# A mixer layer on one core: buffers of four head merges laid elsewhere, and the attention gates kept in halves

## The chip, the cores and the metric

The kernel runs on one core of one Trainium2 chip. The time is what the device needs for one execution, in microseconds (us). The kernel before was timed in three runs: 884.32, 889.29 and 890.98 us, median 889.29. A further run was executed with the hardware profiler on; all rows of the profile come from that one execution.

## The reference, cut to what matters

One layer mixes 1024 latent tokens (width 1024, a grid of 16 rows and 64 columns) with the help of 256 context tokens. It is computed in float32.

```python
h = rmsnorm(x, g_pre) * (1 + scale) + shift          # scale, shift, gate from c (and c_ctx for the context)
na_q, na_k, na_v, na_z, g_qkv, g_z, g_b, g_a = split(h @ w_in)
o_na = neighborhood_attention(na_q, na_k, na_v, ctx_k, ctx_v, rpb)      # 8 heads of 64
q, k, v = l2norm/silu(short_conv(g_qkv)); q, k = axial_rope(q), axial_rope(k)
beta, g = sigmoid(g_b), -exp(A_log) * softplus(g_a + dt_bias)
# gated delta rule, 4 heads of 128, both directions; per chunk of tokens:
a = tril(kb @ k.T * decay, -1);  t_inv = inv(I + a)
u = t_inv @ (v * beta);  w = t_inv @ (kb * exp(gc))
o_g = scan over chunks (state, u, w, q, k), forward + backward
y = concat([o_na * silu(na_z), rmsnorm(o_g) * silu(g_z)]) @ w_out
out = x + gate * rmsnorm(y, g_post)
```

## The kernel before, in words

Every large product is made as three float32r products of high and low parts, so that TensorE works most of the time. The kernel has four stages.

1. **Input and projections** (`phase0`, `phase2`). The modulated input lies transposed in SBUF. Projections of the delta branch go through a short convolution (`conv`, L857, tiles `xp`, `acc`), then to token tiles (`qk_tok`, `qk_back`); `delta_front` (L1004) makes per head the matrices `pm` and `qe` and writes them to DRAM. All these tiles lie in the pool `cv`. A unit triangular 128x128 matrix per head, direction and chunk has to be inverted: `delta_front` copies its four 32x32 diagonal blocks to `ab_dram`, and `inv_blocks` (L1058) inverts them on VectorE (DVE) in 31 steps of two instructions (L1070, L1073). The 320 blocks are handled in three groups (g = 0, 1, 2). Groups 0 and 1 are done within stage 1, group 2 in the next stage; its results go to DRAM as `yd2`, and head 3 alone needs them.

2. **The merges** (`phase_a2`, L1432). While the last projections of the attention (pairs 2 and 3: `pq`, `pk`, `pz`) still run on TensorE (PE), `inv_merge` (L1081) puts the inverted blocks of each of the four heads h together to 128x128 inverses. Its steps are l (load `pmf` from `pm_dram`, and `vl` from `yd`), t (three transposes on DVE: `vx` L1106, `vd` L1107, `ld` L1108, copies into `tm` on ScalarE), z (products `tz`, L1120), u (products `tu`, L1139, whose negatives DVE puts into `tm` and `xo`, L1144), w (products `tz2`, L1153) and e (products `tu2`, results by L1163 and L1164 into `tm`, then two DMAs to `tm_dram`, L1166). The list `MERGES` (L138) gives the order of the steps over the heads. `tm` for direction 0 alternates between `tms[0]` and `tms[1]`; direction 1 has `tms[2]` for all heads, so a head's first write into it waits until the DMA of the head before has read it. `phase_a2` also loads the first attention pair (`na_load`, L562: `kk`, `qh`, `ql`, `gt`, `vv` and the mask `mk`).

3. **Attention and scan** (`phase_b`, L1484). The attention runs in four pairs of heads p = 0 to 3, each in two halves of the queries, rt = 0 and 1, and each half in four column tiles ct. `na_scores`, `na_turn` and `na_values` make the scores, their transposes and the products with the values, which add up in the PSUM tile `po` (one buffer). After the fourth column tile `values` (L620) multiplies the gate tile `zs` by `po` (L627), and `end` (L636) multiplies it by the transposed reciprocal sums, the PSUM tile `prt` (L640, L642), which takes the one buffer of `po` in turn. The result goes to `m_dram` (L646); that of pair 3 stays in SBUF and is split into high and low parts by `split_m` (L708). `zs` is a tile of 1024 queries with one buffer, so pair p + 1 can load it only when both halves of pair p have been written out. Between the attention steps the delta scan (`delta_step`) is called, head by head; `delta_end` (L1293) of a head writes its gated output `zg` to `m_dram` (L1319).

4. **Output projection** (`phase4`): products `py` (L1361 to L1363) over the eight parts k of the mixed width in the order `W_ORDER`, and `out_tile`. Part k = 3 is the result of pair 3.

Engines take their instructions in the order in which the program has them. That order is made by a scheduler of the tile framework, which puts the instructions of each engine in an order by its own estimate of the times; `self.pe` and `self.order` pin some of it. All DMAs above are issued by SyncE (SP), one after the other: a DMA whose buffer isn't free holds all that stand behind it. Pools lie at fixed places in SBUF. The pool `pf` (pair 0 and 2, and borrowed by the merges) and the pool `a2` of the merges (the argument `g3` of `inv_merge`) lie where `cv` was: `a2` takes the addresses where the convolutions' tiles `xp`, `acc` and the token tiles were, the middle and upper parts of `pf` those where the last head's `em`, `pm` and `qe` tiles of `delta_front` were.

## Time and profile before

| | |
|---|---|
| three runs, median | 889.29 us (884.32 to 890.98) |
| the profiled execution | 885.84 us, its span 884.1 us, so 1.7 us outside the span |
| PE busy, share of the span | 829.0 us, 94% |
| DVE, ACT (ScalarE), POOL (GpSimd) | 57%, 47%, 40% |
| granted TensorE clock, mean | 0.968 |
| DMA | 159.65 MB, 181 GB/s on average |

How it is read. PE is busy for 94% of the span, so what a change can give back is for the most part the remaining 55 us in which PE waits, and the time in which PE runs at a lower granted clock. A row of a chain or of waits names what ended a wait; a row of the timeline has the start, the duration, the engine and line, the operation with its tiles, and, in brackets, the idle time before it with what ended it. `SPq` rows are DMAs being issued; the time in them is the issue, not the transfer.

### The profile page before, as it was taken

How to read it: one execution, taken by the hardware profiler on the slowest of the kernel's cores; microseconds unless marked ns; L12 is line 12 of the kernel's file. 1: busy time of each engine (PE TensorE's matmuls, PEld its weight loads, DVE VectorE, ACT ScalarE, POOL GpSimd, SP SyncE). 2: the span in 40 equal slices, each digit the busy share in tenths (PEclk: the TensorE clock that was granted, in tenths of full speed). 3: DMA queues.
4: the chain of work that ended last, by engine and by line, in shares of the span. 5: the costliest groups of instructions: out<-in, count | busy, mean ns of one | idle time of the engine just before them, and what ended most of it. 6: DMA issues, size and time to landing. Idle time of an engine off the chain costs nothing.

```text
span 884.1 us, 16449 instructions
## 1 busy us (share of the span) xinstructions
PE 829.0 (94%) x6082; PEld 701.9 (79%) x6082; DVE 507.9 (57%) x1050; ACT 417.9 (47%) x1086; POOL 357.3 (40%) x430
## 2 busy tenths in 40 slices
PE   5999999999999989898998998999889898989996
PEld 4678887888788768688886887898888787878885
DVE  3454465546626699869819944466466466663342
ACT  5353435744653643464315433666556566753110
POOL 1333231634463461426452103657547468624110
PEclk9999999999999999999998997899999999999999
DMA  9787442264464626543696499986919715123251
GB/s 332 263 274 271 131 132 86 84 214 151 117 204 156 182 85 198 172 121 82 232 244 218 159 265 340 359 190 244 269 56 297 209 60 204 49 108 131 76 194 65
DMA packets 85046, 159.65 MB, mean 181 GB/s; under 512 B 18261, under 2 KB 45222, under 8 KB 82790
## 3 DMA queue, kind: packets, MB, share of 16 engines
q1 hardware_dynamic: 77478, 144.94, 51.4%
q10 hardware_dynamic: 7488, 13.67, 4.8%
q8 instruction: 48, 0.79, 0.4%
q14 instruction: 32, 0.26, 0.1%
HBM read 109.51 MB, written 52.42 MB: 183 GB/s over the span
## 4 chain that ended last, share of the span: by engine, by line
PE 64%; DVE 16%; DMA 13%; issue 3%; ACT 2%; SPq 1%; POOL 0%; DVEq 0%; POOLq 0%; ACTq 0%
PE py L1361 3%; PE py L1362 3%; PE py L1363 3%; DVE tb L1070 3%; DVE vb L1073 2%; PE pa L1252 2%; PE pz L468 2%; PE pz L467 2%; PE pz L463 2%; DMA pm_dram<-pm 2%; PE pa L1263 2%; PE po L781 2%; PE sc L746 2%; DMA tm_dram<-tm 2%; PE po L776 2%
## 5 line engine op out<-in xcount | busy, mean ns | idle before, releaser
L751 ACT ACTIVATE pt<-pt,nm 128x544 f32<-128x544 f32 (+1 forms) x64 | 50.5, 790 | 47.6 <-DVE nm L750 47.3
L750 DVE CUSTOM_DVE_ANT_0 pt<-sc,gm 128x544 f32<-128x544 f32 (+1 forms) x64 | 49.3, 771 | 29.9 <-PE sc L746 25.0
L734 POOL TENSOR_TENSOR gm<-gt,mk 128x288 f32<-128x288 f32 (+1 forms) x48 | 46.5, 972 | 28.7 <-DVE nm L750 28.4
L1224 POOL TENSOR_SCALAR kd<-kt,kd 128x128 f32<-128x128 f32 x72 | 42.7, 605 | 20.6 <-PE pa L1263 19.5
L1012 ACT ACTIVATE em<-em,gc 128x128 f32<-128x128 f32 x80 | 25.5, 391 | 35.3 <-DMA em<-gc_dram 25.8
L467 PE MATMUL pz<-hl,wh_gz 128*128 128x512 f32 x96 | 38.6, 402 | 0.0
L1423 DVE TENSOR_TENSOR finv<-py,ggb 128x512 f32<-128x512 f32 x16 | 10.8, 688 | 47.9 <-ACT finv L1422 47.7
L463 PE MATMUL pz<-hh,wh_gz 128*128 128x512 f32 x96 | 38.3, 399 | 0.0
L468 PE MATMUL pz<-hh,wl_gz 128*128 128x512 f32 x96 | 38.3, 399 | 0.0
L476 PE MATMUL pv<-wh_nv,hh 128*128 128x264 f32 x128 | 35.3, 295 | 2.0 <-ACT hh L265 1.7
L1266 DVE SCALAR_TENSOR_TENSOR s<-s,egl,pa 128x128 f32<-128x128 f32 x64 | 19.7, 344 | 29.3 <-PE pa L1263 29.3
L477 PE MATMUL pv<-wh_nv,hl 128*128 128x264 f32 x128 | 36.5, 290 | 0.0
L1230 POOL TENSOR_SCALAR vb<-v,beta 128x128 f32<-128x128 f32 x40 | 24.2, 604 | 29.9 <-DVE y L1236 27.2
L1031 POOL TENSOR_SCALAR_AFFINE_SELECT qe<-qe 128x256 f32<-128x256 f32 x32 | 25.5, 799 | 25.0 <-DVE qe L1030 24.6
L478 PE MATMUL pv<-wl_nv,hh 128*128 128x264 f32 x128 | 35.4, 286 | 0.0
L879 DVE SCALAR_TENSOR_TENSOR acc_v<-xp_v,cols,acc_v 128x1282 f32<-128x1282 f32 x16 | 29.1, 1817 | 10.8 <-ACT acc_v L877 10.6
L1070 DVE TENSOR_TENSOR tb<-ab,vb 120x31 f32<-120x31 f32 (+15 forms) x62 | 30.2, 487 | 8.6 <-DMA ab<-ab_dram 7.0
L1422 ACT ACTIVATE finv<-py 128x512 f32<-128x512 f32 x16 | 9.5, 598 | 52.9 <-PE py L1363 34.8
L1129 POOL COPY tm<-ld 32x320 f32<-32x320 f32 x16 | 7.3, 454 | 64.1 <-DMA tm_dram<-tm 50.4
L1027 DVE SCALAR_TENSOR_TENSOR pm<-pk,beta,em 128x128 f32<-128x128 f32 x80 | 23.6, 342 | 15.2 <-PE pk L1020 11.0
L764 PE MATMUL tr<-c,pt 128*96 128x128 f32 (+1 forms) x192 | 31.8, 275 | 0.0
L1073 DVE TENSOR_TENSOR vb<-vb,tb 120x31 f32<-120x31 f32 (+15 forms) x62 | 30.1, 486 | 1.6
(432 smaller groups left out, 2865.7 us busy)
## 6 DMA issues: line engine op xcount, KB each, us to landing
wada<-in_w_ada SPq DMA_DIRECT2D x16, 512.0 KB
em<-gc_dram SPq DMA_DIRECT2D x20, 256.0 KB
pm_dram<-pm SPq DMA_DIRECT2D x20, 256.0 KB
tm_dram<-tm SPq DMA_DIRECT2D x8, 640.0 KB
kk<-qk_dram SPq DMA_DIRECT2D x16, 320.0 KB
tm<-tm_dram SPq DMA_DIRECT2D x4, 1280.0 KB
kq_dram<-kq SPq DMA_DIRECT2D x4, 1152.0 KB
kq<-kq_dram SPq DMA_DIRECT2D x4, 1152.0 KB
```

The source lines that it names most:

```text
L463: r = nc.tensor.matmul(ps, wh, xh, start=(k == 0), stop=False)
L467: nc.tensor.matmul(ps, wh, xl, start=False, stop=False)
L468: nc.tensor.matmul(ps, wl, xh, start=False, stop=(k == KC - 1))
L476: nc.tensor.matmul(ps, xh, wh, start=(k == 0), stop=False)
L477: nc.tensor.matmul(ps, xl, wh, start=False, stop=False)
L478: nc.tensor.matmul(ps, xh, wl, start=False, stop=(k == KC - 1))
L734: r = nc.gpsimd.tensor_tensor(self.gm[hh][:, 384 - n:384].rearrange("p (n c r) -> p n c r", c=nco, r=4), gv, self.mk[:, mo:mo + n].rearran ...
L750: nc.vector.tensor_tensor_reduce(pt[:, 384 - n:], sc[:, 512 - n:768], gm[:, 384 - n:], -1.0, 3.0e38, ALU.add, ALU.min, nm)
L751: self.last_exp = nc.scalar.activation(pt[:, 384 - n:], pt[:, 384 - n:], AF.Exp, bias=nm, scale=-1.0, accum_out=sums[:, ct, hh:hh + 1]).in ...
L1070: nc.vector.tensor_tensor(t3, bc(ab[:, 0:m, m:m + 1], [r, m, n]), bc(vb[:, m:m + 1, m:], [r, m, n]), ALU.mult)
L1073: nc.vector.tensor_tensor(vb[:, 0:m, m:], vb[:, 0:m, m:], t3, ALU.subtract)
L1224: r = nc.gpsimd.tensor_scalar(kd[d], kt_[:, t, :], self.kd[:, h, d, t:t + 1], None, ALU.mult)
```

## The change

It has three parts.

- **Merges.** Head 0 now has its tiles in the pool `a2`: `pmf` there (before in `pf`), its block rows in `tms[2]` (before in a `pf` tile), `vx0` in the buffer of `z2`. `tms[2]` is cleared a second time after the transpose. Head 1 takes `kk0` and `kk1` of `pf` for `pmf` (before in `a2`) and `ql0` for `vl1`, head 2 `a2` for `pmf` and the tile `qh1` for its own `vl2` (before it reused head 0's), head 3 uses `vl1` again, and has most of `pmf` in the buffer `vv` of `pf`, in which group 2 is inverted, and the rest in a buffer of `vd`. The loads of `pmf` now stand after those of `vl` in the text. Their sizes and the arithmetic are unchanged.
- **Gates.** `zs` becomes two tiles of 512 queries, one for each rt. After `end` of a half, that half is written to `m_dram`, and the same half of the next pair is loaded.
- **Pair 3.** `split_m` splits each half as it is finished.

```diff
--- before.py
+++ after.py
@@ -604,18 +604,23 @@
         def load(p):
             qk, gts, vv = self.na_pairs.pop(p) if p in self.na_pairs else self.na_load(na, p)
             self.na_first = self.na_first or self.last_load
-            zs = na.tile([P, S], F32, name=f"zs{p}", tag="zs", bufs=1)
-            self.load(zs, self.z_dram[P * p:P * p + P, :])
             self.na_last = self.last_load
-            return qk, gts, vv, zs
+            return qk, gts, vv
+
+
+        def load_z(p, rt):
+            zs[p, rt] = na.tile([P, 512], F32, name=f"zs{p}_{rt}", tag=f"zs{rt}", bufs=1)
+            self.load(zs[p, rt], self.z_dram[P * p:P * p + P, 512 * rt:512 * rt + 512])
 
         self.gms, self.gmi = [self.nw.tile([P, 640], F32, name=f"gm{i}") for i in range(3)], 0
         for g in self.gms:
             nc.gpsimd.memset(g[:, 384:], 0.0)
-        pairs = {0: load(0)}
+        pairs, zs = {0: load(0)}, {}
+        for rt in range(2):
+            load_z(0, rt)
         units = [(p, rt, ct) for p in range(4) for rt in range(2) for ct in range(4)]
         sums, po, rb, turned, scores = {}, {}, {}, {}, {}
-        row = lambda p, rt: pairs[p][3][:, 512 * rt:512 * rt + 512].rearrange("p (a t c) -> p a t c", a=8, t=4)
+        row = lambda p, rt: zs[p, rt].rearrange("p (a t c) -> p a t c", a=8, t=4)
 
         def values(j):
             p, rt, ct = units[j]
@@ -640,12 +645,13 @@
                 self.pe(nc.tensor.transpose(pt[:, ct * P:(ct + 1) * P],
                                             rb[j][:, 2 * ct:2 * ct + 2, :].rearrange("p a b -> p (a b)"), self.ident))
             nc.vector.tensor_tensor(row(p, rt), pt.rearrange("p (t a c) -> p a t c", t=4, a=8), row(p, rt), ALU.mult)
+            if p < 3:
+                self.load(self.m_dram[P * p:P * p + P, 512 * rt:512 * rt + 512], zs[p, rt])
+                load_z(p + 1, rt)
+            else:
+                self.split_m(3, zs[p, rt], 512 * rt)
             if rt == 0:
                 return
-            if p < 3:
-                self.load(self.m_dram[P * p:P * p + P, :], pairs[p][3])
-            else:
-                self.split_m(3, pairs[p][3])
             if p == 2:
                 self.clock += 4
                 w = [self.pf.tile([P, n], F32, name=f"early_{t}", tag=t)[:, :D]
@@ -705,17 +711,19 @@
             nc.gpsimd.tensor_tensor(lo.bitcast(F32R), raw, hi, ALU.subtract)
             self.load_pieces()
 
-    def split_m(self, k, z):
-        nc = self.nc
-        if k == 3:
-            w = self.g3.tile([P, 18, P], F32, name=f"m{k}", tag="kq", bufs=2).rearrange("p t c -> p (t c)")
-            hi, lo = w[:, :D], w[:, D:2 * D]
-        else:
-            hi, lo = (self.g3.tile([P, 10, P], F32, name=f"m{c}{k}", tag="kt", bufs=2).rearrange("p t c -> p (t c)")[:, :D]
-                      for c in "hl")
-        nc.scalar.copy(hi.bitcast(F32R), z)
-        nc.vector.tensor_tensor(lo.bitcast(F32R), z, hi, ALU.subtract)
-        self.ms[k] = (hi.bitcast(F32R), lo.bitcast(F32R))
+    def split_m(self, k, z, o=0):
+        nc = self.nc
+        if k not in self.ms:
+            if k == 3:
+                w = self.g3.tile([P, 18, P], F32, name=f"m{k}", tag="kq", bufs=2).rearrange("p t c -> p (t c)")
+                w = w[:, :D], w[:, D:2 * D]
+            else:
+                w = [self.g3.tile([P, 10, P], F32, name=f"m{c}{k}", tag="kt", bufs=2).rearrange("p t c -> p (t c)")[:, :D]
+                     for c in "hl"]
+            self.ms[k] = tuple(v.bitcast(F32R) for v in w)
+        hi, lo = (v[:, o:o + z.shape[1]] for v in self.ms[k])
+        nc.scalar.copy(hi, z)
+        nc.vector.tensor_tensor(lo, z, hi.bitcast(F32), ALU.subtract)
 
     def na_scores(self, ps, p, rt, ct, hh, pair, sums):
 
@@ -1080,30 +1088,45 @@
 
     def inv_merge(self, g3, ps, h):
         nc = self.nc
-        pm = []
-        for d in range(2):
-            pool, tag = (g3, f"pm{d}") if h % 2 else (self.pf, f"kk{d}")
-            pm.append(pool.tile([P, 10, P], F32, name=f"pmf{h}_{d}", tag=tag))
-            nc.sync.dma_start(pm[d][0:96], self.pm_dram[h][0:96, d])
         if h == 0:
 
-            self.vls = [self.pf.tile([P, S], F32, name=f"vl{i}", tag=f"q{c}") for i, c in enumerate(("l0", "h1"))]
             self.tms = [g3.tile([P, 10, P], F32, name=f"tm{i}") for i in range(3)]
             self.xo = g3.tile([P, 10, 64], F32, name="xo")
-            for w in (*self.vls, *self.tms, self.xo):
+            for w in (self.tms[2], *self.tms[:2], self.xo):
                 nc.gpsimd.memset(w, 0.0)
-        vl = self.vls[h % 2]
+            self.vls = [self.tms[2].rearrange("p t c -> p (t c)")[:, :S]]
+        elif h < 3:
+            self.vls.append(self.pf.tile([P, S], F32, name=f"vl{h}", tag=("ql0", "qh1")[h - 1]))
+            nc.gpsimd.memset(self.vls[h], 0.0)
+        else:
+            self.vls.append(self.vls[1])
+        vl = self.vls[h]
         for b in range(4):
             g, i = divmod(8 * h + 2 * b, 12)
             nc.sync.dma_start(vl[32 * b:32 * b + 20], self.yd[g][10 * i:10 * i + 20].rearrange("t j i -> t (j i)"))
         vd, ld = (g3.tile([P, 2, 10, 32], F32, name=f"{c}d{h}", tag=f"{c}d", bufs=2) for c in "vl")
 
+        if h < 3:
+            pieces = [(d, 0, (self.pf.tile([P, 10, P], F32, name=f"pmf{h}_{d}", tag=f"kk{d}") if h == 1 else
+                              g3.tile([P, 10, P], F32, name=f"pmf{h}_{d}", tag=f"pm{d}", bufs=1))) for d in range(2)]
+        else:
+            w = self.pf.tile([P, 2 * S], F32, name="pmf3", tag="vv").rearrange("p (t c) -> p t c", c=P)
+            pieces = [(0, 0, w[:, :10]), (1, 0, w[:, 10:15]),
+                      (1, 5, g3.tile([P, 5, P], F32, name="pmf3_1", tag="vd", bufs=2))]
+        pm = {}
+        for d, t0, w in pieces:
+            nc.sync.dma_start(w[0:96], self.pm_dram[h][0:96, d, t0:t0 + w.shape[1]])
+            pm.update({(d, t0 + t): w[:, t] for t in range(w.shape[1])})
+
         xo = self.xo
         tm = [self.tms[h % 2], self.tms[2]]
         yield
-        vx = self.pf.tile([P, S], F32, name=f"vx{h}", tag="ql1")
+        vx = self.pf.tile([P, S], F32, name=f"vx{h}", tag="ql1") if h else g3.tile([P, 1280], F32, name="vx0", tag="z2",
+                                                                               bufs=1)[:, :S]
         flat = lambda w: w.rearrange("p d t c -> p (d t c)")
         nc.vector.transpose(vx, vl)
+        if h == 0:
+            nc.gpsimd.memset(self.tms[2], 0.0)
         nc.vector.transpose(flat(vd), vx.rearrange("p (j s) -> p s j", s=32)[:, :20])
         nc.vector.transpose(flat(ld), flat(vd))
         cp = nc.scalar.copy
@@ -1117,7 +1140,7 @@
             for t in range(10):
                 for b in (0, 2):
                     s1, s2 = slice(32 * b, 32 * b + 32), slice(32 * b + 32, 32 * b + 64)
-                    nc.tensor.matmul(pz[s2, t, :], pm[d][s1, t, s2], ld[s1, d, t, :], start=True, stop=True,
+                    nc.tensor.matmul(pz[s2, t, :], pm[d, t][s1, s2], ld[s1, d, t, :], start=True, stop=True,
                                      tile_position=(32 * b, 32 * b + 32))
             for b in (0, 2):
                 s2 = slice(32 * b + 32, 32 * b + 64)
@@ -1150,7 +1173,7 @@
             pz = ps.tile([P, 8, 64], F32, name=f"tz2{h}_{d}{t0}", tag="ta", bufs=3)
             for t in range(n):
                 lo = xo[A, t0 + t, :] if d == 0 else tm[1][A, t0 + t, A]
-                nc.tensor.matmul(pz[B, t, :], pm[d][A, t0 + t, B], lo, start=True, stop=True, tile_position=(0, 64))
+                nc.tensor.matmul(pz[B, t, :], pm[d, t0 + t][A, B], lo, start=True, stop=True, tile_position=(0, 64))
             nc.scalar.copy(z2[B, d, t0:t0 + n], pz[B, :n])
         yield
         for t0 in (0, 5):
```

The first instruction that stands elsewhere lies in the merges; what comes before is in the same order on all engines. Three places show what is moved. The first is DVE at the start of the merges (numbers at the end of names are buffer numbers; L1070 and L1073 before are L1078 and L1081 now, `tb2` and `ab_vv` are group 2's tiles). Before:

```order
L529 TENSOR_TENSOR sl_k20_4641<-pk2_0_4615,sh_k20_4640 128x512
L1070 TENSOR_TENSOR tb2_qh0_4370<-ab_vv_4368 80x31
L1073 TENSOR_TENSOR ab_vv_4368<-ab_vv_4368,tb2_qh0_4370 80x31
L1070 TENSOR_TENSOR tb2_qh0_4370<-ab_vv_4368 80x60
L1073 TENSOR_TENSOR ab_vv_4368<-ab_vv_4368,tb2_qh0_4370 80x30x2
L1070 TENSOR_TENSOR tb2_qh0_4370<-ab_vv_4368 80x87
L1073 TENSOR_TENSOR ab_vv_4368<-ab_vv_4368,tb2_qh0_4370 80x29x3
L1070 TENSOR_TENSOR tb2_qh0_4370<-ab_vv_4368 80x112
L1106 STREAM_TRANSPOSE vx0_4405<-vl0_4387 128x1024
L1073 TENSOR_TENSOR ab_vv_4368<-ab_vv_4368,tb2_qh0_4370 80x28x4
L529 TENSOR_TENSOR sl_k21_4759<-pk2_1_4733,sh_k21_4758 128x512
L1107 STREAM_TRANSPOSE vd0_4403<-vx0_4405 128x640
```

Now:

```order
L529 TENSOR_TENSOR sl_k20_4640<-pk2_0_4614,sh_k20_4639 128x512
L1127 STREAM_TRANSPOSE vx1_4606<-vl1_4410 128x1024
L1127 STREAM_TRANSPOSE vx0_4401<-tm2_4385 128x1024
L1078 TENSOR_TENSOR tb2_qh0_4370<-ab_vv_4368 80x31
L1130 STREAM_TRANSPOSE vd0_4395<-vx0_4401 128x640
L1130 STREAM_TRANSPOSE vd1_4416<-vx1_4606 128x640
L1081 TENSOR_TENSOR ab_vv_4368<-ab_vv_4368,tb2_qh0_4370 80x31
L1131 STREAM_TRANSPOSE ld0_4396<-vd0_4395 128x640
L1131 STREAM_TRANSPOSE ld1_4417<-vd1_4416 128x640
L1078 TENSOR_TENSOR tb2_qh0_4370<-ab_vv_4368 80x60
L1127 STREAM_TRANSPOSE vx2_4904<-vl2_4692 128x1024
L1081 TENSOR_TENSOR ab_vv_4368<-ab_vv_4368,tb2_qh0_4370 80x30x2
```

The first transposes of heads 1 and 0 have moved ahead of group 2, and that of head 2 now stands, twelve rows higher than before, behind group 2's second product; `sl_k21`, which empties a PSUM buffer of the projections, has moved down by eight rows.

The second place is SP where group 2's results are written and read back. Before:

```order
L1087 DMA pmf3_0_4985<-pm_dram3_76 96x1280
L1079 DMA yd2_4952<-ab_vv_4368 80x1024
L156 DMA qh0_0_5376<-qk_dram_93 64x1024 x2
L1098 DMA vl1_4388<-yd2_4952 20x1024 x4
L1087 DMA pmf3_1_4987<-pm_dram3_76 96x1280
L156 DMA vv0_5395<-v_dram_116 96x4x128
L156 DMA vv0_5395<-v_dram_116 128x4x128 x2
L156 DMA vv0_5395<-v_dram_116 96x4x128
L156 DMA qh0_1_5385<-qk_dram_93 64x1024 x2
L1166 DMA tm_dram1_86<-tm1_4390 128x1280
L156 DMA ql0_1_5388<-qk_dram_93 64x1024
L1166 DMA tm_dram1_86<-tm2_4391 128x1280
```

Now:

```order
L532 DMA qk_dram_93<-sh_k30_5597 128x512
L533 DMA qk_dram_93<-sl_k30_5598 128x512
L1087 DMA yd2_4953<-ab_vv_4368 80x1024
L156 DMA qh0_0_5378<-qk_dram_93 64x1024 x2
L156 DMA kk0_1_5384<-qk_dram_93 64x1280
L1106 DMA vl1_4410<-yd2_4953 20x1024 x4
L1118 DMA pmf3_4992<-pm_dram3_76 96x1280
L1118 DMA pmf3_4992<-pm_dram3_76 96x640
L1189 DMA tm_dram1_86<-tm1_4384 128x1280
L1189 DMA tm_dram1_86<-tm2_4385 128x1280
L156 DMA kk0_1_5384<-qk_dram_93 64x1280
L156 DMA ql0_0_5381<-qk_dram_93 64x1024 x2
```

The four loads of `vv0` and those of `qh0_1` no longer stand between `yd2` and the second write of `tm_dram1`. `qh0_1` has moved up to the masks, `kk0` up to here and into the rows before; `pmf3`, all but its last five chunks, now follows `yd2`; `vv0` has moved down behind the scan's `kq0` and `zg0`.

The third place is SP in pair 0 and pair 1, at the gates. Before:

```order
L156 DMA vv2_6700<-v_dram_116 128x4x128 x2
L156 DMA vv2_6700<-v_dram_116 96x4x128
L1319 DMA m_dram_96<-zg0_6551 128x1024
L156 DMA zs1_5902<-z_dram_95 128x1024
L1296 DMA zg1_7361<-z_dram_95 128x1024
L156 DMA kt3_7606<-kt_dram3_80 128x1280
L156 DMA v3_7605<-vt_dram3_84 128x1280
```

Now, at the end of pair 0's first half:

```order
L156 DMA vv1_5901<-v_dram_116 128x4x128 x2
L156 DMA vv1_5901<-v_dram_116 96x4x128
L156 DMA m_dram_96<-zs0_0_5726 128x512
L156 DMA zs1_0_6219<-z_dram_95 128x512
L156 DMA kt2_6811<-kt_dram2_79 128x1280
L156 DMA v2_6810<-vt_dram2_83 128x1280
```

and in pair 1:

```order
L156 DMA vv2_6707<-v_dram_116 96x4x128
L1342 DMA m_dram_96<-zg0_6556 128x1024
L156 DMA zs1_1_6618<-z_dram_95 128x512
L1319 DMA zg1_7369<-z_dram_95 128x1024
L156 DMA m_dram_96<-zs1_0_6219 128x512
L156 DMA zs2_0_7044<-z_dram_95 128x512
L156 DMA kt3_7614<-kt_dram3_80 128x1280
```

The load of pair 1's first half of the gates has moved up by 15 rows, out from behind the scan's write of `zg0`, and only the second half's stands there now.

## The prediction

> **What bounds the kernel now.** I read the page first, then the busy time by stretches from the merges on.
>
> ```profile
> span 884.1 us, 16449 instructions
> ...
> PE 829.0 (94%) x6082; PEld 701.9 (79%) x6082; DVE 507.9 (57%) x1050; ACT 417.9 (47%) x1086; POOL 357.3 (40%) x430
> ```
>
> ```profile
> 440.00:480.00 40.00, 36.91 (x347) 30.24 (x346) 20.25 (x43) 13.31 (x27) 16.66 (x21) 0.91 0.88 255
> 480.00:520.00 40.00, 38.51 (x558) 31.99 (x546) 30.83 (x69) 15.29 (x33) 4.60 (x6) 0.96 0.55 171
> 520.00:552.00 32.00, 29.27 (x533) 25.40 (x533) 14.17 (x27) 10.69 (x24) 7.18 (x14) 0.82 1.00 325
> 552.00:635.00 83.00, 80.42 (x740) 72.83 (x740) 47.85 (x150) 53.19 (x160) 53.19 (x75) 0.97 0.86 264
> 635.00:700.00 65.00, 56.91 (x528) 52.20 (x526) 33.21 (x105) 36.40 (x114) 35.05 (x50) 0.97 0.72 210
> ```
>
> The columns after the length are the busy times of PE, its weight loads, DVE, ACT and POOL, then the granted clock, the DMA share and GB/s. PE is the bound of the attention: 80.4 of 83 us at 552 to 635. It isn't at 635 to 700, where 8.1 us are missing, and at 520 to 552 the DMA engines are full (share 1.00, 325 GB/s) while PE's clock is 0.82. Next I asked what PE waited for from 552 to the end, and followed the chain of waits.
>
> ```profile
> PE prt L640 <- DVE zs L627: 8.0, 2, 4.2
> ...
> PE py L1361 <- DVE zs L642: 1.6, 1, 1.6
> PE pa L1263 <- ACT vn L1257: 1.2, 2, 0.8
> PE ot L1311 <- DVE o L1308: 1.2, 1, 1.2
> ```
>
> ```profile
> 457.02 7.81 DMA vl<-yd
> ...
> 471.42 3.95 DMA vl<-yd
> ...
> 510.01 4.66 DMA yd<-ab_vv
> ...
> 515.75 2.97 DMA vl<-yd
> ...
> 523.29 8.94 DMA tm_dram<-tm
> ...
> 538.73 6.43 DMA tm_dram<-tm
> ...
> 551.45 0.72 PE sc L743 x2
> ...
> 635.31 6.64 DMA zs<-z_dram
> ...
> 693.75 6.75 DMA zs<-z_dram
> ```
>
> So two things stand on the chain that the change touches: two loads of the gates (635.31 and 693.75), and two writes of head inverses (8.94 and 6.43 us for 640 KB each) ahead of the first score at 551.45.
>
> **The gates in halves.** Why the load is late stands in SP's timeline; what it costs, in PE's.
>
> ```profile
> 615.83 0.33 SPq L156 DMA_DIRECT2D m_dram<-zs  x1
> ...
> 632.91 2.36 SPq L1319 DMA_DIRECT2D m_dram<-zg  x1
> 635.31 0.63 SPq L156 DMA_DIRECT2D zs<-z_dram  x1
> ```
>
> ```profile
> 584.62 0.60 PE L640 MATMUL prt<-c,rb 128*128 128x128 f32 x4
> ...
> 642.81 1.09 PE L640 MATMUL prt<-c,rb 128*128 128x128 f32 x4 [4.20 <-DVE zs L627]
> 644.90 1.12 PE L776 MATMUL po<-tcx,vcx 128*64 128x128 f32 x8
> ...
> 692.17 0.66 PE L776 MATMUL po<-tcx,vcx 128*64 128x128 f32 x8
> ...
> 701.35 1.09 PE L640 MATMUL prt<-c,rb 128*128 128x128 f32 x4 [3.76 <-DVE zs L627]
> ```
>
> Pair 0's gates were written out at 615.83; pair 1's load came 19 us later, because SP first had to issue the scan's `zg`. Now the first half is loaded after pair 0's first half, whose `prt` stands at 584.62, 54 us before PE's wait began (642.81 - 4.20): with a load as slow as the ones above (6.75) it is there 47 us early. The second half still stands behind `zg` (632.91), but is used half a pair later, about 29 us (half of 693.75 - 635.31). So both PE waits go: 4.20 + 3.76 = 8.0 us. Behind the wait the same eight products take 1.12 instead of 0.66 us, so PE runs slowly for a while: I take 0.5 us for each wait, 1.0 in all. Next late is PE itself. Sum: **-9.0**, between -7.4 (if reciprocals are then 0.3 us late at each place) and -11.
>
> [...]
>
> The price is 7 more DMAs, four loads and three writes, each one issue of SP (0.33), between rows in which SP waits anyway; nothing that they hold is used within 10 us. [...]
>
> **The merges.** At their start PE waits, and is then slow.
>
> ```profile
> 467.95 0.50 PE L463 MATMUL pq<-hh,wh_nq 128*128 128x512 f32 x1 [1.47 <-DVE sl_k L529]
> 470.07 2.35 PE L1120 MATMUL tz<-ld,pmf 32*32 32x32 f32 x80 [1.62 <-DVE ld L1108]
> ...
> 473.80 0.63 PE L467 MATMUL pq<-hl,wh_nq 128*128 128x512 f32 x1
> ...
> 476.74 0.40 PE L467 MATMUL pq<-hl,wh_nq 128*128 128x512 f32 x1
> ```
>
> ```profile
> 462.81 0.21 DVE L1070 TENSOR_TENSOR tb_qh<-ab_vv 80x31 f32<-80x31 f32 x1 [11.63 <-DMA ab_vv<-ab_dram]
> ```
>
> Although head 0's new places are free early, the order keeps its loads behind the last writes of the stage before: SP still issues `ab_dram` first, then head 1's `pmf` and only then head 0's `vl` and `pmf`. What changes is small. Two `pmf` loads less lie ahead of group 2 and of head 0's `vl`: 2 x 480 KB at 255 GB/s = 3.9 us. DVE, idle for 11.63 us, can take `vx1` and `vx0` while it waits, and `ld0`, which held `tz`, comes at about 466 instead of 470. Against it `sl_k21` comes later on DVE, and PE reaches `tz` twelve matmuls sooner, so part of the wait only moves. I take -2 for this start.
>
> The end is where more is to be had. Projections end on PE and DMA writes hold DVE:
>
> ```profile
> 532.61 0.51 PE L468 MATMUL pz<-hh,wl_gz 128*128 128x512 f32 x1
> ```
>
> ```profile
> 532.33 0.48 DVE L1144 TENSOR_SCALAR tm<-tu 32x320 f32<-32x320 f32 x1 [4.82 <-DMA tm_dram<-tm]
> ...
> 545.29 0.48 DVE L1144 TENSOR_SCALAR tm<-tu 32x320 f32<-32x320 f32 x1 [4.64 <-DMA tm_dram<-tm]
> ```
>
> The write at 523.29 took 8.94 us because `vv0` (0.92 MB), half of `ql0_1`, `qh0_1` (0.52 MB) and its twin (0.66 MB) went ahead: with its own 0.66 MB 3.0 MB, 9.3 us at 325 GB/s. Without `vv0`, `qh0_1` and `ql0_1`, but with 0.74 MB of `pmf3`, it is 2.05 MB, 6.3 us, and its issue comes at about 518, since nothing of `vv0` is issued in front. So it lands near 525 instead of 532.2, and head 2's later steps run beside the projections, in which the order now also has four groups of small products that stood behind them. PE gets through the projections at about 532.5 as before: 2 us sooner by the start, some 2 us later by those products. What is left is head 2's last step, head 3's u, w and e. Before, this went from about 537.3 (the group just ahead of the write at 538.73) to 551.45, 14 us. In it the write took 6.43, with 1.3 MB of `kk0` ahead, which is now loaded earlier; two writes of 0.66 MB alone are 4.0 us at 325. So 14 - 2.4 = 11.7, and the first score comes at 544 to 546: I take **-6** for the merges in all, start included. Bounds: -12 (the 9.5 us of both DVE waits and more of the slow clock) to +4 (below).
>
> Now `vv0` waits on SP for head 3's last products `tz2`, and behind it wait `qe0`, `tm1`, `v1` and head 3's writes. Its cover: about 4.3 MB of the scan's loads go ahead from about 537, 13 us, then its own 0.92 MB, 2.8 us, so it is complete at about 553 and its first quarter at 551. The first use was
>
> ```profile
> 560.15 0.66 PE po L781 x12
> ```
>
> and comes at 554 now. It holds by 1 to 3 us; if it doesn't, that comes off the -6. The second clearing of `tms[2]` lies on POOL, 0.40 busy and not on the chain there.
>
> **Pair 3.** Its first half is split while the attention goes on, so that the products of k = 3 for the first four token tiles no longer wait for the last gate. The waits of 1.6 (`py`) and 1.2 (`ot`) may go, -2.8. But the last `po` multiplication now stands behind the scan's two `o` products on DVE, and more `py` products stand on PE ahead of the scan's last step: up to +3.5. I take -0.5, since PE has the moved products to do in either case.
>
> Sum: -9.0 - 6 - 0.5 = -15.5. From the profiled 885.84 (span 884.1) that is 870.3. The median of the runs is 3.45 above the profiled execution; with the same offset **874**.
>
> **Rivals.** *Only the gates.* The merges come out even, as the loads start no earlier and PE, in order, meets `tz` before its data: -9 to -9.5, 880. For it: the order of SP and the +4 above. Against it: the full DMA stretch loses 2 MB ahead of the write on the chain.
>
> *The merges give more.* If head 3's steps keep PE at full clock (0.82 now) and both DVE waits go, they give -12 and the ends -1: 867.
>
> *Slower: DVE held at the third row of its new order.* `vx2` stands behind group 2's second product, and its `vl2` comes last of eleven loads. Every us that it lands after about 466 holds all of group 2 behind it and, by `sl_k21`, PE. By the chain the last `vl` landed at 471.42 + 3.95 = 475.4: then the merges lose about 10 and gain 6, the bound of +4, and the kernel is at 884. At 481 the gates' 9 are used up as well; at 490, where it could be if the DMA queue keeps head 0's `pmf` and everything else in front, it is 898. For it: SP's order, and a DMA share of 0.88. Against it: only 3.2 MB are in front, 457.02 + 7.81 = 464.8 was the landing behind 2.9 MB.
>
> **Chances.** The forecast 0.48 (869 to 879), more from the merges 0.14 (863 to 869), only the gates 0.28 (878 to 885, of this 0.10 below 880.4), DVE held 0.10 (885 to 905, of this 0.06 above 898). A measurement of this kernel tells about 1% from no change, that is 880.4 and 898.2. Faster: 0.48 + 0.14 + 0.10 = 0.72; the same 0.22; slower 0.06. The range leaves out the slow rival and half of the fast one: 865 to 885.
>
> **What would show it.** The waits of `prt` for `zs` gone, no `zs` load on the chain; DVE's waits for `tm_dram` under 3 us each; the first score at 543 to 547 instead of 551.45; `po` L781 without a DMA wait for `vv0`; the wait of `py` for the last gate under 1 us. It is wrong if PE has a new wait of over 3 us at `tz` or `pq` near 463 to 476, if DVE stands before `vx2`, or if the attention, without its two waits, still takes as long because another wait comes at the same places.

## The result, and the profile after

The changed kernel takes 874.98 us (median of 6 runs, 871.0 to 878.37) against 887.25 us for the kernel before (6 runs, 884.32 to 890.98): the ratio is 0.986, with a 95% interval of 0.982 to 0.990. The forecast was 874. The total was met, but two of its three terms, the merges and pair 3, were not, and the errors nearly cancel. The rows that answer to those of before, first the page and the same stretches:

```profile
span 874.9 us, 16467 instructions
...
PE 826.5 (94%) x6082; PEld 699.6 (80%) x6082; DVE 507.0 (58%) x1051; ACT 417.9 (48%) x1087; POOL 359.9 (41%) x431
```

```profile
520.00:552.00 32.00, 28.61 (x506) 23.85 (x505) 13.61 (x23) 10.70 (x25) 3.95 (x10) 0.91 0.77 245
552.00:635.00 83.00, 80.41 (x731) 72.93 (x730) 46.41 (x143) 50.48 (x152) 52.20 (x74) 0.93 0.95 289
635.00:700.00 65.00, 63.12 (x610) 58.04 (x608) 40.61 (x127) 41.80 (x130) 39.94 (x56) 1.00 0.81 231
```

At 635 to 700 PE is busy for 63.1 of 65 us instead of 56.9, and its clock is 1.00 instead of 0.97: there the two loads of the gates stood. At 520 to 552 the DMA engines are no longer full (0.77 instead of 1.00), but PE has not gained anything by it (28.6 us busy instead of 29.3). What PE waits for after 552, of the changed kernel:

```profile
PE pa L1275 <- DVE y L1259: 4.5, 9, 1.6
PE prt L645 <- DVE zs L632: 1.7, 1, 1.7
...
PE py L1384 <- DVE zs L647: 0.2, 1, 0.2
```

The two waits of `prt` for the gates (4.20 and 3.76 us) are gone; a `prt` wait of 1.7 us is new, at the end of pair 3. The chain of waits at the end of the merges:

```profile
540.25 0.23 PE pz L468
...
543.12 0.51 DVE tm L1187
543.67 5.78 DMA tm_dram<-tm
...
549.55 0.49 DVE tm L1167
...
555.73 0.72 PE sc L751 x2
```

The projections now end at 540.5 instead of 533.1, a write of `tm_dram` still stands on the chain, and the first score comes at 555.7, 4.3 us later than before (551.4) and not 6 us sooner. Of these 4.3 us, 1.7 are there at the end of stage 1 already, in which nothing was changed.

To see where the time went I cut every profile at the same instructions: the last `sl_q` of stage 1 on DVE, the first score on PE, and then the DVE instructions that write `pt` (the row maxima of the scores; 64 of them, 16 for each pair, 8 for each half). The stretches between their starts (the last one up to the end of the last `py`), in us, for the 14 profiles of this study; the last column is the median time of all runs of a kernel:

| kernel | stage 1 up to last `sl_q` | merges, to first score | to pair 1's second half | to pair 2's second half (1st stop) | to pair 3 (2nd stop) | to pair 3's second half | to the last `py` | time |
|---|---|---|---|---|---|---|---|---|
| before | 443.9 | 107.47 | 79.14 | 59.04 | 32.96 | 29.63 | 125.01 | 887.25 |
| before, again | 442.3 | 107.92 | 79.12 | 58.85 | 32.66 | 28.58 | 125.63 | 883.69 (one run) |
| changed | 445.6 | 110.04 | 79.71 | 53.75 | 27.70 | 27.93 | 123.19 | 874.98 |
| changed, again | 445.7 | 110.01 | 79.65 | 53.75 | 27.71 | 26.86 | 123.16 | 874.59 |
| gates alone | 443.0 | 110.41 | 79.23 | 53.61 | 27.71 | 27.97 | 123.17 | 873.07 |
| merges alone | 443.6 | 109.47 | 79.88 | 59.91 | 34.85 | 29.36 | 123.70 | 889.66 |
| changed, split whole | 443.2 | 110.43 | 79.75 | 53.76 | 27.71 | 26.85 | 123.18 | 876.11 |
| before, load in halves | 442.5 | 108.36 | 78.95 | 58.65 | 35.30 | 29.58 | 125.24 | 887.38 (one run) |
| changed, own `tm3` | 444.1 | 106.24 | 80.76 | 53.58 | 27.71 | 27.96 | 124.69 | 872.05 |
| the same, merges first | 444.4 | 111.21 | 86.85 | 53.60 | 27.69 | 27.97 | 124.60 | 883.84 |
| gates alone, `raw` tied | 442.7 | 109.96 | 79.52 | 53.63 | 27.71 | 26.74 | 123.20 | 874.21 |
| own `tm3`, `vv` first | 444.7 | 109.00 | 83.50 | 53.64 | 27.71 | 26.97 | 123.19 | 874.32 |
| before, `raw` early | 445.7 | 109.84 | 79.44 | 59.37 | 35.45 | 27.95 | 124.15 | 888.15 |
| own `tm3`, `zg` later | 443.2 | 106.82 | 79.97 | 53.60 | 27.70 | 27.00 | 123.18 | 870.68 |

In the columns of the two stops the kernels with halves agree within 0.2 us; stage 1, in which nothing was changed, varies by 3.4 us, and the merges by 3 us at one and the same order. The first two profiles therefore mislead on the merges, and the runs below had to settle that.

### The profile page after: what moved, and what is told of

The parts are those of the page before. It is cut to its first block, busy times and chain, and to the rows that moved or that the text cites. A ratio compares the mean times of both kernels' runs of the same rounds, so it can differ in the third digit from the quotient of the medians.

```text
span 874.9 us, 16467 instructions
## 1 busy us (share of the span) xinstructions
PE 826.5 (94%) x6082; PEld 699.6 (80%) x6082; DVE 507.0 (58%) x1051; ACT 417.9 (48%) x1087; POOL 359.9 (41%) x431
## 4 chain that ended last, share of the span: by engine, by line
PE 71%; DVE 14%; DMA 7%; ACT 3%; issue 3%; SPq 1%; POOL 0%; DVEq 0%; POOLq 0%; ACTq 0%
PE py L1384 3%; PE py L1385 3%; PE py L1386 3%; PE pz L463 3%; PE pz L468 3%; PE pz L467 3%; DVE tb L1078 3%; PE pa L1275 3%; DVE vb L1081 2%; PE po L789 2%; PE pa L1286 2%; PE po L784 2%; PE tr L772 2%; DMA pm_dram<-pm 2%; PE sc L754 2%
## 5 line engine op out<-in xcount | busy, mean ns | idle before, releaser
L1078 DVE TENSOR_TENSOR tb<-ab,vb 120x31 f32<-120x31 f32 (+15 forms) x62 | 32.1, 518 | 9.3 <-DMA ab<-ab_dram 7.7
L1039 POOL TENSOR_SCALAR_AFFINE_SELECT qe<-qe 128x256 f32<-128x256 f32 x32 | 25.5, 799 | 24.9 <-DVE qe L1038 24.4
L887 DVE SCALAR_TENSOR_TENSOR acc_v<-xp_v,cols,acc_v 128x1282 f32<-128x1282 f32 x16 | 29.1, 1817 | 10.9 <-ACT acc_v L885 10.6
L1446 DVE TENSOR_TENSOR finv<-py,ggb 128x512 f32<-128x512 f32 x16 | 10.9, 689 | 42.0 <-ACT finv L1445 41.9
L1035 DVE SCALAR_TENSOR_TENSOR pm<-pk,beta,em 128x128 f32<-128x128 f32 x80 | 23.6, 343 | 15.5 <-PE pk L1028 11.5
L770 ACT COPY tcx<-tc 128x256 f32<-128x256 f32 x64 | 23.5, 367 | 16.2 <-PE tc L768 15.8
L449 POOL TENSOR_TENSOR wl_gz<-wr_gz,wh_gz 128x512 fp32r<-128x512 f32 x12 | 16.4, 1370 | 35.4 <-ACT wh_gz L448 24.5
```

Source lines behind the costliest of these rows:

```text
L1078: nc.vector.tensor_tensor(t3, bc(ab[:, 0:m, m:m + 1], [r, m, n]), bc(vb[:, m:m + 1, m:], [r, m, n]), ALU.mult)
```

## The experiments

**The parts apart.** The theory from the two traces (A) against the terms of the forecast (B). First the changed kernel again, with nothing edited:

> The changed kernel itself again, as the mark for the runs beside it. Both theories: 875 us, 12 us (1.4%) under the kernel before.

It took 874.59 us, ratio 0.985 (0.982 to 0.987). Then the gates and the split of pair 3 put into the kernel before, with `inv_merge` left alone:

> The kernel before with the gates in halves and the split of pair 3 in halves, and with the merges as before. Theory A (read from the two traces: the gates gave 10.6, pair 3 gave 3.5, the merges cost 2.6): 14 us under before, ratio 0.984, so about 2.6 us under the changed kernel. Theory B (the forecast's terms: gates -9.0, pair 3 -0.5, merges -6): 9.5 us under before, ratio 0.989, so about 6 us over the changed kernel. In its trace both waits of prt for the gates (4.20 and 3.76) are gone and the first score stands at 551.4, as before.

It took 873.07 us, ratio 0.982 (0.979 to 0.984): 15.1 us under before (888.15 in the runs beside it). Theory A holds: the gates, with the split of pair 3, carry all of the gain. And the change of `inv_merge` alone, with the gates as before:

> The kernel before with the merges' part alone, the gates as before. Theory A: 1 to 3 us over before, ratio 1.001 to 1.003, with the first score 2 to 4 us later than 551.4 and both waits for the gates as before. Theory B: 6 us under before, ratio 0.993.

It took 889.66 us, ratio 1.002 (1.000 to 1.004). The merges give nothing: +1.5 us alone, an interval that begins at no change, and +1.5 between the gates alone and the whole change (873.07 and 874.59), whose intervals overlap. The two add up: -15.1 + 1.5 = -13.6, as the whole change measures (888.15 to 874.59). The expected place was not quite met: in the profile of the gates alone the first score came at 553.4, although up to there every engine has its instructions in the order of before. Over the profiles of the table that have the merges of before (107.47, 107.92, 110.41, 108.36, 109.96, 109.84) the mean is 109.0, over the four with the changed merges and no further edit there (110.04, 110.01, 109.47, 110.43) it is 110.0; the stretch behind gives another 0.5 (79.2 and 79.7). That is 1.5 us as well, though not in each profile: in that of the merges alone the two stops are longer too (59.91 and 34.85) and the last stretch is shorter.

**The split of pair 3 undone.** In the changed kernel:

```diff
-            else:
-                self.split_m(3, zs[p, rt], 512 * rt)
             if rt == 0:
                 return
+            if p == 3:
+                for half in range(2):
+                    self.split_m(3, zs[3, half], 512 * half)
```

> The changed kernel with the halves of pair 3 split into high and low parts only when both are finished, as before (four instructions of 512 columns at the end instead of two after each half). Theory A: the split in halves lets the output products of the first token tiles run while the last gate is still open, worth the 3.5 us of pair 3, so 878 here, ratio to before 0.990. Theory B: worth 0.5 us, so this run is within 1 us of the changed kernel and what pair 3 gained comes from elsewhere.

It took 876.11 us, ratio 0.986 (0.984 to 0.988), 1.5 us over the changed kernel but with intervals that overlap. Its trace decides: from pair 3's start on it takes 26.85 + 123.18 us, the changed kernel beside it 26.86 + 123.16. That is theory B: the split gives nothing that a profile shows, and what pair 3 gained comes with the gates' tiles.

**The kernel before again**, for a second profile of the merges.

> The kernel before once more, for a second profile of its merges. Between the last write of q of the first stage (sl_q) and the first score, the kernel before took 107.47 us in its profile, the gates alone with the same order 110.41, and the four with the changed merges 109.5 to 110.4. Theory A (the merges cost 2.6): 107.5 again. Theory C (they cost nothing, and the first profile of before was a quick one): 109 to 111.

The stretch took 107.92 us, near to theory A; but the gates alone (110.41) have the same order, so one profile says little here, and only the mean above and the medians carry the 1.5 us.

**Halves for the load alone.** In the kernel before, the tile and the writes as they were:

```diff
-            self.load(zs, self.z_dram[P * p:P * p + P, :])
+            for o in (0, 512):
+                self.load(zs[:, o:o + 512], self.z_dram[P * p:P * p + P, o:o + 512])
```

> The kernel before with each load of the gates made as two loads of 512 queries into the same tile of 1024; they stand where the one load stood, and everything is written out as before. The first half should land 2 to 3 us sooner than the whole one did, so prt waits some 2 us and some 1.5 us instead of 4.20 and 3.76. [...] If the first half lands no sooner, nothing changes.

The waits of PE at 630 to 730 in this kernel:

```profile
PE pa L1253 <- DVE y L1237: 7.1, 4, 5.8
PE prt L641 <- DVE zs L628: 3.9, 1, 3.9
```

The first half landed hardly sooner: 3.9 us of waiting instead of 4.20 in pair 1, and in pair 2 a stop of 5.8 us, since DVE stood in front of the gates with the scan's `y` behind them. The stretches come out 0.2 us shorter and 2.6 us longer than in the kernel before again. The stops were not short enough to show what a shorter stop costs beside its wait. The run does say something else: smaller transfers in the same place give nothing here. What counts in this kernel is that the first half's load was moved out from behind `zg`. In the changed kernel:

```profile
602.58 0.33 SPq L156 DMA_DIRECT2D zs<-z_dram  x1
...
637.28 2.47 SPq L1342 DMA_DIRECT2D m_dram<-zg  x1
639.79 0.56 SPq L156 DMA_DIRECT2D zs<-z_dram  x1
```

**The write of head 2 taken off the tail.** Direction 1 of head 3 gets a tile of its own, in the buffer of head 2's `pmf`:

```diff
-        tm = [self.tms[h % 2], self.tms[2]]
+        tm = [self.tms[h % 2], self.tms[2] if h < 3 else g3.tile([P, 10, P], F32, name="tm3", tag="pm0", bufs=1)]
+        if h == 3:
+            nc.gpsimd.memset(tm[1], 0.0)
```

> The changed kernel with a tile of its own for direction 1 of head 3 (in the buffer of head 2's pmf, cleared once more), so that head 3's first writes into it no longer wait until head 2's has gone to DRAM; PE, ACT and SP have the same order but for one group of five products. Theory W (the tail of the merges hangs on that write, 543.67 + 5.78): head 3's steps go on at 545 instead of 549.6, the first score comes 4 to 5 us sooner, 870 us. Theory O (PE in its order and the other transfers are next at once): 1 us or less, 874.

It took 872.05 us, ratio 0.982 (0.980 to 0.985). Theory W holds up to the first score: the merges take 106.24 instead of 110.04 us, and DVE goes on with head 3 at once (rows below). The 3.8 us are those of one profile; the two later kernels with this tile take 109.00 and 106.82 in the table. The tail alone, from the end of the last projection to the first score, is steadier: 12.3 us here and 12.1 and 10.9 in those two, 14.9 to 15.3 in the four profiles of the changed merges. The tile is worth about 3 us there.

```profile
541.50 0.48 DVE L1169 TENSOR_SCALAR tm<-tu 32x320 f32<-32x320 f32 x1 [0.28 <-PE tu L1164]
541.99 0.48 DVE L1169 TENSOR_SCALAR xo<-tu 32x320 f32<-32x320 f32 x1
542.51 1.00 DVE L1169 TENSOR_SCALAR tm<-tu 32x320 f32<-32x320 f32 x2
```

But from the first softmax to the ninth, where it took 24.3 us (557.09 to 581.37), it takes 25.3, for a wait that the prediction had named as the limit of the merges' gain, `vv0` behind the scan's loads:

```profile
558.84 0.66 PE L784 MATMUL po<-tcx,vcx 128*64 128x128 f32 x8
560.57 0.66 PE L789 MATMUL po<-tl,vv 96*64 96x128 f32 x8 [1.07 <-DMA vv<-v_dram]
```

**More weight for the merges' steps**, on top of it:

```diff
-                            with tc.high_priority(offset=200):
+                            with tc.high_priority(offset=400):
```

> The same, and the merges' steps given more weight over the projections (400 instead of 200 in the scheduler's priority), by which 15 products of pz stand behind head 2's last transposes on PE instead of 6, and head 0's first products stand four groups of projections earlier. Theory W: PE has projections to do while head 2's last and head 3's steps pass through the other engines, 1 to 3 us less than the run with the tile alone, 867 to 869. Theory O: the earlier start waits longer for head 0's transposes (3 us and more at tz already), which eats that up or more: 870 to 876.

It took 883.84 us, ratio 0.994 (0.990 to 0.998), with ten runs spread from 875.96 to 887.52; the profile is that of a long one (885.10). Neither theory had this: more of the projections stand late, so `z_dram` is written late, SP comes to the loads of pair 0 and the scan late, and the scan's first products wait. The first two rows of PE's waits at 553 to 595:

```profile
PE pa L1277 <- POOL vb L1255: 2.9, 1, 2.9
PE pa L1277 <- DMA v<-vt_dram: 2.7, 1, 2.7
```

The stretch behind the first score takes 86.85 instead of 80.76 us. What is gained on PE's order is lost on SP's.

**`vv0` ahead of `kq`**, on the kernel with its own `tm3` and the weight of before:

```diff
-            if h or i >= 4:
+            if h or i >= 3:
                 self.gate = self.na_first
```

> The changed kernel with head 3's own tile, and the scan's first load of kq (1.18 MB) put behind vv0 on SP; nothing else moves. Theory V (with its own tile the first po products, 1.07 us late for vv0 and at the low clock for longer, gave back 1.65 of the 3.8 us of the merges): vv0 lands before 560, the wait is gone, and the time is 1 to 1.7 us under the run with the tile alone (872.05), 870.4 to 871. Theory K (kq is then late instead, for the first product of the scan at 556): a new wait of PE for kq of 1 us or more, 872 or over.

It took 874.32 us, ratio 0.987 (0.984 to 0.990). Theory K holds; the wait for `vv` is gone, and a longer one takes its place:

```profile
566.44 0.68 PE L1259 MATMUL pa<-s,kq 128*128 128x128 f32 x4 [3.06 <-DMA kq<-kq_dram]
```

**`zg` behind them instead**, which nobody needs there:

```diff
-        nc.sync.dma_start(zg, self.z_dram[512 + P * h:512 + P * h + P, :])
+        self.load(zg, self.z_dram[512 + P * h:512 + P * h + P, :], self.na_first if h == 0 else None)
```

> The changed kernel with head 3's own tile, and the load of the scan's zg (0.5 MB, used 60 us later) put behind vv0 and the scan's next loads; kq stays ahead of vv0. Theory V: vv0 lands 1.2 to 1.5 us sooner, the wait of 1.07 for it goes, and kq is not late: 1 to 1.6 us under the run with the tile alone, about 871. Theory D (the DMA engines are full there, and PE waits for the next transfer instead): the stretch from the first to the ninth softmax stays at 25.3 us, where the kernel before took 23.7, and the time at 872.

It took 870.68 us, ratio 0.982 (0.979 to 0.985). From the first to the ninth softmax it takes 24.4 us instead of 25.3; neither wait is left:

```profile
558.63 0.66 PE L784 MATMUL po<-tcx,vcx 128*64 128x128 f32 x8
559.27 0.88 PE L789 MATMUL po<-tl,vv 96*64 96x128 f32 x12
560.08 0.71 PE L1259 MATMUL pa<-s,kq 128*128 128x128 f32 x4
```

Theory V holds for the place. The time does not show it: the median is the lowest of all versions, but the ratio of 0.982 to the kernel before is also that of the tile alone and of the gates alone.

**What pair 3 gained.** The table shows a second gain of the gates that the forecast had not: up to pair 3's second half it is 26.7 to 28.0 us in all kernels with halves, 28.6 to 29.6 in the four with whole gates and the loads of before. In the kernel before, ScalarE stands in front of a cast of the output weights (`raw`), whose loads SP issues behind the load of pair 3's gates, and the scan's `vn` stands behind that cast:

```profile
733.86 0.32 SPq L156 DMA_DIRECT2D zs<-z_dram  x1
734.23 0.90 SPq L156 DMA_DIRECT2D raw<-in_w_out  x2
```

```profile
738.86 0.62 ACT L704 CAST early_o<-raw 128x512 fp32r<-128x512 f32 x1 [1.37 <-DMA raw<-in_w_out]
739.38 0.26 ACT L1257 COPY vn<-pa 128x128 f32<-128x128 f32 x1
```

This is in the code: the loads of `raw` are tied behind `self.na_last`, and in `load` that was the load of the gates; since `load` no longer loads them, it is the last load of `vv`. The first run ties them back, in the gates alone:

```diff
             self.load(zs[p, rt], self.z_dram[P * p:P * p + P, 512 * rt:512 * rt + 512])
+            self.na_last = self.last_load
```

> The gates alone, with one thing put back: in the kernel before, the loads of the output weights (raw) were tied behind the last load of the gates, and with the gates in halves they are tied behind the last load of vv instead. Here they are tied behind the last half of the gates again: on SP the first two loads of raw stand five rows later, after that half, and nothing else moves. Theory L (part of what pair 3 gained is ScalarE's cast of these weights, which waited for raw in the kernel before and held the scan's vn behind it): the cast waits 1 to 2 us for its DMA again, the stretch from the first score softmax of pair 3 to that of its second half grows from 28.0 to 29.5 us or more, 1.5 to 2.5 us over the gates alone (873.07), so about 875. Theory M (that stretch differs by chance): within 0.5 us of the gates alone in that stretch.

It took 874.21 us, ratio 0.987 (0.983 to 0.991), and the stretch took 26.74 us. But the tie reaches only pair 3's first half, not the second as the expectation had it, so the two loads still went out ahead of pair 2's second write and the cast waited for nothing. The run does not test the theory. The other way round it can be tested, in the kernel before:

```diff
+            self.na_last = self.last_load
             zs = na.tile([P, S], F32, name=f"zs{p}", tag="zs", bufs=1)
             self.load(zs, self.z_dram[P * p:P * p + P, :])
-            self.na_last = self.last_load
```

> The kernel before, with the loads of the output weights tied behind pair 3's last load of vv instead of behind pair 3's load of the gates, as they are tied since the gates are in halves; merges and gates as before. The first two loads of raw now stand ahead of pair 2's write of its gates, and ScalarE has the casts in the order of the changed kernel. Theory L: the cast no longer waits for its DMA (1.4 us before), and the stretch from the first softmax of pair 3 to that of its second half is 27 to 28 us, as in the kernels with halves, instead of 28.6 to 29.6: 1.5 to 2 us under before, about 886. Theory M (the stretch is shorter for another reason, such as the gates' shorter transfers): 28.6 to 29.6 us, and the time is that of before.

The stretch is 27.95 us, as theory L has it, and the cast waits for nothing:

```profile
740.59 0.60 ACT L704 CAST early_o<-raw 128x512 fp32r<-128x512 f32 x1
```

The time does not follow: 888.15 us, ratio 1.002 (0.999 to 1.004). The two loads now stand ahead of the load of pair 2's gates too, and that is what PE waits for at 690 to 730:

```profile
PE prt L640 <- DVE zs L627: 5.3, 1, 5.3
```

5.3 instead of 3.76 us, and the stretch of the second stop takes 35.45 instead of 32.7 to 33.0. So the tie is shown, by this one run, to be the cause of the shorter stretch; that it is worth something in time needs gates which do not wait.

## Why the prediction was right, and where it was wrong

**The gates, -9.0: right in kind, too small.** Both waits went, and the two stretches are 5.29 and 5.26 us shorter, 10.6 in all, inside the bounds of -7.4 to -11, the latter an estimate for which no run shows a term. The waits themselves were 8.0. What was mis-sized is the slow time behind each, which I took at 0.5 us; it is, by difference, 1.1 (5.29 - 4.20) and 1.5 (5.26 - 3.76); the second profile of the kernel before gives 0.9 and 1.5. The clock in the kernel before, a microsecond to each row from 642 on, shows it:

```profile
642.00:643.00 1.00, 0.19 (x1) 0.22 (x2) 1.00 (x2) 0.00 (x0) 0.00 (x0) 0.91 0.79 279
643.00:644.00 1.00, 1.00 (x6) 1.00 (x6) 1.00 (x5) 0.50 (x1) 0.00 (x0) 0.50 0.42 168
644.00:645.00 1.00, 1.00 (x6) 0.56 (x7) 0.72 (x2) 1.00 (x5) 0.00 (x0) 0.50 0.00 0
645.00:646.00 1.00, 1.00 (x10) 1.00 (x12) 0.89 (x3) 0.31 (x2) 0.00 (x0) 0.50 0.00 0
646.00:647.00 1.00, 1.00 (x16) 0.83 (x13) 0.15 (x1) 0.92 (x2) 0.00 (x0) 0.88 0.06 16
647.00:648.00 1.00, 1.00 (x11) 1.00 (x11) 0.61 (x2) 0.26 (x1) 0.00 (x0) 1.00 0.00 0
```

The number behind the five engines, the clock, is 0.50 from about 642.8 to 646.2, 3.4 us. The mean of 0.97 at 635 to 700 before is no sign of a shorter slow time: 3.4 us at 0.50 in 65 us make a mean of 0.974, and the second slow time (700.9 to 704.3) lies behind the end of that stretch. Two such times of 3.4 us at half clock come to 1.7 us each, an estimate from these rows, and 8.0 + 3.4 = 11.4 is more than the 10.6 measured; why it is less was not tried. The last section has a fall of the clock without such a stop. The seven additional transfers cost nothing that a stretch shows: up to pair 1's second half the gates alone take 79.23 us, the kernel before 79.14 and 79.12.

**The merges, -6: they gave nothing, +1.5.** The step that failed is "PE gets through the projections at about 532.5 as before". They ended at 540.5. Counted from the last `sl_q`, so without stage 1, the last projection ends after 89.2 to 91.6 us (mean 90.3) in the six profiles with the merges of before and after 94.4 to 95.5 (94.9) in the four with the changed ones and no further edit there. The tail from there to the first score takes 18.3 to 18.9 us (18.6) and 14.9 to 15.3 (15.1). So 3.5 us were gained in the tail, and 4.5 lost ahead of it. Up to its last projection PE now makes some 70 more of the merges' small products (851 instead of 780), and it is idle for 6.0 to 8.3 us instead of 3.5 to 4.9.

The first half of the mechanism came in part. Head 1's write, without `vv0` and `qh0` in front, was issued at 522.0 and landed at 529.9; before it was 523.3 and 532.2, and 518 and 525 were worked out. DVE's waits for `tm_dram`, 4.82 and 4.64 us before, are 0.65 us at the one place that is left. But DVE now stands 4.89 us in front of head 3's `vx` (2.37 before), whose `vl` comes from group 2, and the last step of group 2 comes 68.4 to 69.5 us after the last `sl_q` instead of 65.6 to 67.7. And PE, in its order, had projections in front of head 2's last products, from 531.5 to 536.1 and from 538.8 to 540.5, and DVE waited for the products behind them, 2.4 and 3.9 us. From DVE's timeline of the changed kernel:

```profile
524.76 1.25 DVE L1127 STREAM_TRANSPOSE vx<-vl 128x1024 f32<-128x1024 f32 x1 [4.89 <-DMA vl<-yd]
...
541.24 0.49 DVE L1187 TENSOR_SCALAR tm<-tu 64x320 f32<-64x320 f32 x1 [3.88 <-PE tu L1184]
...
549.55 0.48 DVE L1167 TENSOR_SCALAR tm<-tu 32x320 f32<-32x320 f32 x1 [0.65 <-DMA tm_dram<-tm]
```

PE did the same work in another order. The tail got shorter, from 18.3 to 15.2 us in the first two profiles, though not to the 11.7 that I worked out: head 2's write was still on it, issued at 543.67 instead of 538.73 and 5.78 us long. That it was, and what it is worth, was shown by the tile of its own: about 3 us. At the start of the merges PE waits 3.05 us for head 0's transposes (before, 1.47 and 1.62 at two places), where the sum had -2:

```profile
469.14 1.45 PE L1143 MATMUL tz<-ld,pmf 32*32 32x32 f32 x80 [3.05 <-DVE ld L1131]
```

The row that I had named for "wrong" (a wait of over 3 us at `tz`) came true; in the other three profiles of the changed merges the wait is 3.3 to 6.8 us. The rival "only the gates", at 880, had PE meet `tz` before its data, and the merges even. It was right on the merges, but its mechanism is only a part of what happened: the other part is the small products and the waits for head 2 and head 3 further on. The rival with DVE held in front of `vx2` did not come: it waited 1.2 us there.

**Pair 3, -0.5: too small, and for another reason.** From pair 3's second half to the last `py` the kernels with halves take 123.2 in seven profiles and 124.6 and 124.7 in two, those without 123.7 to 125.6; the means differ by 1.2 us. The `ot` wait (1.17) is gone, and the wait of 1.65 stands at another place, now in front of `prt`. The split in halves has no part in it. A good part of the difference is the clock: behind these waits it is at 0.50 for 3.4 us (789.6 to 793.0 in the kernel before) in the five profiles that take 124.6 us or more with halves and 125.0 or more without, and in none of the others. Without this slow time it is 123.2 with halves and 123.70 and 124.15 without, so at the same clock the gates gave 0.5 to 1.0 us here. What the forecast missed altogether is the 1.9 us up to pair 3's second half (means 29.3 and 27.4), by a load that was tied to the load of the gates in the code. The chain of before showed it (the write of the gates at 730.91, the load of `raw` at 734.23, the cast at 738.86), but I read the chain only where the change had a line.

**The sum.** Forecast -9.0 - 6 - 0.5 = -15.5; by the runs -10.6 - 1.9 - 1.2 + 1.5 = -12.2, while the medians give -12.3 in the first comparison and -13.6 in the second. That 874 was met is luck: gates and pair 3 gave 4.2 us more than forecast and the merges 7.5 less, and the median of 889.29 from which the forecast started was 1 to 3 us above those of the kernel before in the later comparisons (885.85 to 888.15).

## What to carry to other kernels

Here a load that waited behind another engine's result on a DMA queue was cured by moving its issue (the waits of 4.20 and 3.76 us went, and the stretches are 5.29 and 5.26 us shorter), for which its buffer had to come free sooner; cutting the transfer without moving it gave nothing (waits of 3.9 and 5.8 us were left). When a wait of another engine is taken away in front of an engine that takes its work in order and is busy for 94% of the span, as PE is here, look up in the order what that engine does in the meantime: here it did the work that had filled the tail, and the tail only moved (3.5 us gained in it, 4.5 lost ahead of it). And when a load is removed from a function, look for what was tied behind it.

## What was not expected of the hardware

PE's clock also fell without a long stop, to 0.50 in the kernel with its own `tm3`:

```profile
546.00:548.00 2.00, 2.00 (x34) 2.00 (x33) 0.48 (x1) 0.63 (x2) 0.00 (x0) 0.50 1.05 345
548.00:550.00 2.00, 2.00 (x23) 1.86 (x22) 0.98 (x2) 0.21 (x1) 0.00 (x0) 0.50 0.89 362
```

PE reads as busy for all of these 4 us, the gaps in the 4 us ahead of them were 0.34 and 0.98, and the clock stays at 0.50 from 544 to 556. The work there is the merges' products of 64x64 and the waits between them; the same stretch of the kernel before ran at 0.52 (540 to 550). Whether the size of the products or the sum of the short gaps does it was not tried.

Nor did the same wait always have the same effect. The `prt` wait of pair 3 stands, at 1.64 to 1.67 us, in all nine kernels with halves. In seven of them the clock stays at 1.00 behind it, in two (the own `tm3`, and the same with the merges first) it is at 0.50 for 3.4 us. These two are the ones that take 124.7 and 124.6 us up to the last `py`, where the seven take 123.2. The wait and a row behind it, in the changed kernel and then with its own `tm3`:

```profile
785.42 0.63 PE L645 MATMUL prt<-c,rb 128*128 128x128 f32 x4 [1.67 <-DVE zs L632]
788.00:789.00 1.00, 1.00 (x6) 0.80 (x5) 0.60 (x2) 1.00 (x2) 0.00 (x0) 1.00 0.00 0
```

```profile
781.00 0.63 PE L645 MATMUL prt<-c,rb 128*128 128x128 f32 x4 [1.64 <-DVE zs L632]
784.00:785.00 1.00, 1.00 (x4) 0.81 (x3) 0.87 (x1) 1.00 (x3) 0.00 (x0) 0.50 0.00 0
```

After the long stops the clock fell too. In the kernel before it is at 0.50 for 3.4 us behind the stop of 4.20 us, and for 3.4 us behind that of 3.76. With the merges alone its mean is 0.97 over the 59.91 us of the first stop's stretch and 0.90 over the 34.85 of the second's, with `raw` early 0.90 over the 35.45 us around the stop of 5.3: some 3.6, 7.0 and 7.1 us at half clock, estimated from mean and length. That is not in proportion to the stop (3.4 us behind one of 4.20, some 7 behind one of 5.3). What decides was not tried.
